# A two-layer decoder step: GpSimd's splits in pieces of 128 columns, the sample's SSD step in full tiles, no GpSimd work around the second norm

## The chip, the cores and the metric

The kernel runs on one core of one Trainium2 chip. The metric is the device time of one execution in microseconds (us). A core has engines that run their own instruction streams and wait for each other on semaphores: TensorE (PE in the profile; PEld is its loading of weights), VectorE (DVE), ScalarE (ACT), GpSimd (POOL) and SyncE (SP), whose queue issues almost all of the DMA transfers here.

## The reference

One inference step of a decoder of two layers, for a prompt of 1024 tokens and 8 sample sequences of one token each, whose 8192 past tokens lie in a paged cache. Cut to what matters:

```
def trunk_layer(x, c, ...):
    shift1, scale1, gate1, shift2, scale2, gate2 = split(silu(c) @ w_ada + b_ada)
    h = rmsnorm(x, g_norm1) * (1 + scale1) + shift1
    z, xbc, dt_raw, cq, ckv, kpe, u = split(h @ w_in)
    ssd_out, hT, conv_new = ssd_mixer(z, xbc, dt_raw, conv_buf, h0, ...)   # 6 heads x 64, state 128, 2 groups
    mla_out = rmsnorm(attend(q, lat, kpe_r), g_mla_out)                     # latent attention, 6 heads
    pool_out, pool_new = pool_mixer(u, pool_buf, ...)
    x = x + gate1 * (concat(ssd_out, mla_out, pool_out) @ w_out)
    h2 = rmsnorm(x, g_norm2) * (1 + scale2) + shift2
    x = x + gate2 * ((silu(h2 @ w_gate) * (h2 @ w_up)) @ w_down)            # 1024 -> 2816 -> 1024
    return x, lat, kpe_r, hT, conv_new, pool_new
```

For a sample sequence the SSD step is one token long: the new state is exp(dt A) h0 + B (dt x), the output is C times the new state, plus D x. All arithmetic is float32.

## The kernel before

Activations lie transposed, features on the 128 partitions and the 1032 tokens (1024 of the prompt, then the 8 of the sample) in columns. A float32 product is made of three matmuls: each operand is cut into a high part that ScalarE rounds (line 88) and the rest, which VectorE or GpSimd makes by a subtraction (line 89, or 1141 for the cached pages); `gemm` and `mm3` then sum high x high, low x high and high x low (lines 133 to 135). So each weight tile and each activation tile that TensorE uses costs one ScalarE copy and one subtraction, and the constants at the end of the file say which subtractions GpSimd makes.

Each layer has these stages, with the times of layer 0 in the profiled execution: the first norm and the input projection (0 to 270 us); a weave (270 to 990) of generators that take turns: `sample` (the attention of the eight sample sequences over their pages, split by `smp_split` in tiles of 4 x 128 columns), and beside it one after another `ssd_prompt`, `ssd_sample`, `ssd_finish` and `mla_prompt`, and blocks of the adaLN product; the output projection and the second norm (990 to about 1200); the up passes of the FFN with a seven-product scheme (to 1600); the down passes (to 1845). Layer 1 repeats this.

`ssd_sample` takes the eight sequences in four steps (two groups g, two halves q of four sequences). A step scales the old state by a decay (line 668, on GpSimd), adds the outer product of B and dt x (line 665, operands of 8 rows), and `product` multiplies the new state with one column of C for each sequence (lines 637 to 641, one column streamed).

`out_proj` goes over the two halves g of the tokens, and in each over eight tiles m of the output features: it loads the weight tile i + 2 and splits tile i + 1 ahead (`out_load`, `out_conv`; OPV lists the tiles that VectorE splits, GpSimd the others), multiplies, adds the gated result to x (line 1411), squares it and sums the squares (line 1423, GpSimd where m is even). `norm_half` makes the second norm of half g: `fresh` multiplies four of the tiles by the reciprocal root (line 1457) and applies scale and shift column block by column block (line 1462 on VectorE for the blocks in XFV, line 1465 on ScalarE for the others); `cut` splits them into X for the FFN (on GpSimd for the blocks in XPL); sums and differences of blocks follow (line 1481). It runs for half 0 while `out_proj` works on half 1. `up_first` loads the first up and gate weights and prepares WAH = 3 of their operands; `up_conv` prepares one (sums of blocks at line 1538, on GpSimd for those in WPS in the first four passes and in WPT later; then a split, on GpSimd for those in WPF and WPL). The first four passes take one half of the tokens each, the later ones both.

Tiles come from two pools: `C` gives one of NA = 24 slots of 128 x 1032, `B` one of 20. A tile that finds no free slot waits until an older one is released. The Tile framework schedules each engine's instructions; the order follows the order of issue in the text with priorities, so the engines' order can change with the change.

Of the kernel before, what the change touches and what calls it, by code (L numbers as in the profile page):

```python
# [17 lines left out]
TP = 1024  # L18
NB = 8
# [29 lines left out]
class Net:  # L49
# [36 lines left out]
    def split(self, x, h, l, eng=None):  # L86
        nc = self.nc
        nc.scalar.copy(h, x)  # L88
        (eng or nc.gpsimd).tensor_tensor(out=l, in0=x, in1=h.bitcast(F32), op=ALU.subtract)  # L89
# [345 lines left out]
    def softplus(self, l):  # L435
# [43 lines left out]
        ea = self.ea = self.S([6, NB], "ea", bufs=1)  # L479
        nc.scalar.activation(out=ea, in_=p[0:6, 128 - NB:128], func=AF.Exp)  # L480
# [5 lines left out]
    def ssd_prompt(self, l):  # L486
# [9 lines left out]
        def decays(c):  # L496
# [10 lines left out]
            for g in range(2):  # L507
# [14 lines left out]
                if c:  # L522
                    nc.scalar.activation(out=E[:, 384 * g:384 * g + 384], in_=df[:, 0:384], func=AF.Exp)
                    (nc.gpsimd if g in PE6 else nc.vector).tensor_tensor(
                        out=e6[:, 3 * g:3 * g + 3, :], in0=e6[:, 3 * g:3 * g + 3, :],
                        in1=Cf[g][:, s].unsqueeze(1).to_broadcast([128, 3, 128]), op=ALU.mult)
# [10 lines left out]
        for c in range(8):  # L537
# [9 lines left out]
            for g in range(2):  # L547
                (nc.gpsimd if g in PM6 else nc.vector).tensor_tensor(
                    out=m6[:, 3 * g:3 * g + 3, :], in0=m6[:, 3 * g:3 * g + 3, :],
                    in1=gm[:, g, :].unsqueeze(1).to_broadcast([128, 3, 128]), op=ALU.mult)  # L550
# [44 lines left out]
    def ssd_sample(self, l):  # L595
# [7 lines left out]
        for h in range(6):  # L603
            nc.tensor.matmul(p[:, NB * h:NB * h + NB], self.K(K_ID + h, 1, r1=6).to_broadcast([6, 128]), ea,
                             start=True, stop=True)
        px = self.Gp()
        for i in range(3):
            for e in range(2):
                nc.tensor.matmul(px[64 * e:64 * e + 64, NB * i:NB * i + NB],
                                 self.K(K_ID + 64 + 2 * i + e, 1, 64, 70).to_broadcast([6, 64]), acr[64:70, TP:],  # L610
                                 start=True, stop=True)
        eb = self.S([128, 6, NB], "eb", bufs=1)
        nc.vector.tensor_copy(eb, p[:, 0:48].rearrange("p (h b) -> p h b", h=6))
        xd = self.S([128, 3, NB], "xd", bufs=1)
        for i in range(3):
            nc.vector.tensor_tensor(out=xd[:, i, :], in0=x[i][:, TP:], in1=px[:, NB * i:NB * i + NB],
                                    op=ALU.mult)
        yield 3
        p = self.Gp()
        for i in range(3):  # L620
            nc.tensor.transpose(p[0:NB, 128 * i:128 * i + 128], xd[:, i, :], self.K(K_ID, 128))
        xn = self.C(name="xnb")[0:NB, 0:384]
        nc.vector.tensor_copy(xn, p[0:NB, 0:384])
        p = self.Gp()
        for g in range(2):
            nc.tensor.transpose(p[0:NB, 128 * g:128 * g + 128], Bf[g][:, TP:], self.K(K_ID, 128))
        bn = self.C(name="bnb")[0:NB, 0:256]
        nc.vector.tensor_copy(bn, p[0:NB, 0:256])
        yield 3
        ysb = self.S([128, 24], "ysb", bufs=1)  # L630
        def product(g, q, h1):
            yp = self.Gp()
            for b in range(4):
                o = 192 * b
                cc = Cf[g][:, TP + 4 * q + b:TP + 4 * q + b + 1]
                if g == 0:
                    nc.tensor.matmul(yp[:, b:b + 1], h1[:, o:o + 128], cc, start=True, stop=True)
                    nc.tensor.matmul(yp[0:64, 4 + b:5 + b], h1[:, o + 128:o + 192], cc, start=True, stop=True)
                else:
                    nc.tensor.matmul(yp[64:128, b:b + 1], h1[:, o:o + 64], cc, start=True, stop=True)  # L640
                    nc.tensor.matmul(yp[:, 4 + b:5 + b], h1[:, o + 64:o + 192], cc, start=True, stop=True)
            for j, r, a in (((0, slice(0, 128), 0), (1, slice(0, 64), 4)) if g == 0 else
                            ((1, slice(64, 128), 0), (2, slice(0, 128), 4))):
                nc.vector.tensor_copy(ysb[r, 8 * j + 4 * q:8 * j + 4 * q + 4], yp[r, a:a + 4])

        pend = None
        def state(i):
# [5 lines left out]
        for g in range(2):  # L653
            for q in range(2):

                rhs, h1 = self.C(name="hr"), self.C(name="h1")
                if g + q < 2:
                    state(2 * g + q + 1)
                nc.vector.tensor_tensor(
                    out=rhs[0:NB, 0:768].rearrange("p (b e) -> p b e", b=4),  # L660
                    in0=xn[:, 192 * g:192 * g + 192].unsqueeze(1).to_broadcast([NB, 4, 192]),
                    in1=self.K(K_ID + 4 * q, 4, r1=NB).unsqueeze(2).to_broadcast([NB, 4, 192]), op=ALU.mult)
                d = [self.Gp() for _ in range(2)]
                for a in range(2):
                    nc.tensor.matmul(d[a][:, 0:384], bn[:, 128 * g:128 * g + 128], rhs[0:NB, 384 * a:384 * a + 384],
# [18 lines left out]
        yield  # L684
        for j in range(3):
            nc.vector.scalar_tensor_tensor(out=self.y[j][:, TP:], in0=x[j][:, TP:], scalar=self.V(l, V_DSK + j),
                                           in1=ysb[:, 8 * j:8 * j + 8], op0=ALU.mult, op1=ALU.add)
# [443 lines left out]
    def smp_split(self, page):  # L1131
# [9 lines left out]
        nc.gpsimd.tensor_tensor(out=ll, in0=v, in1=lh.bitcast(F32), op=ALU.subtract)  # L1141
# [229 lines left out]
    def out_proj(self, l, mod, xsrc, side):  # L1371
# [6 lines left out]
        for i, (g, m) in enumerate(todo):  # L1378
# [7 lines left out]
            if g:  # L1386
                for _ in range(SDO):
                    next(side[0], None)
            if i == 1:
# [32 lines left out]
            else:  # L1422
                (nc.vector if m % 2 else nc.gpsimd).tensor_tensor(out=sqs[z], in0=sqs[z], in1=sq, op=ALU.add)
# [136 lines left out]
    def up_first(self, l):  # L1560
# [5 lines left out]
        for j in range(WAH):  # L1566
            self.up_conv(l, j)

    def ffn(self, l, X, mod, side, sink):
# [10 lines left out]
        done = WAH + WA0  # L1580
        for j in range(7 * len(self.passes)):
            while done <= j + WAH:
# [428 lines left out]
```

## Time and profile before

| | |
|---|---|
| time, median of 3 runs | 3662.61 us (3662.19 to 3663.1) |
| the profiled execution's own time | 3663.35 us |
| its span in the profile | 3661.6 us |
| busy: TensorE, VectorE, ScalarE, GpSimd | 3436.4, 2358.1, 1732.6, 1546.8 us |
| mean granted clock of TensorE | 0.962 |
| GpSimd instructions | 1173 |

The profile is of one execution, and its span leaves 1.75 us of that execution's time outside. Busy times count each engine alone; the engines work side by side. The clock is that of TensorE as a share of 2.4 GHz, of which 0.5 is the lower of its two levels.

### The profile page before, as it was taken

Reading aid. Unit: us, or ns where it says so; the run is one execution under the profiler, and the core shown is the slowest. Engines: PE = TensorE matmul, PEld = TensorE weight load, DVE = VectorE, ACT = ScalarE, POOL = GpSimd, SP = SyncE. Lnnn points to the kernel's source line nnn. Section 1 sums busy time; section 2 is a strip of 40 time slices with the busy share of each in tenths; the row PEclk is TensorE's granted clock in tenths of the full one; section 3 lists DMA queues with packets and bytes.
Section 4 is the critical chain, followed back from the end, with each engine's and each line's share of the span. In section 5 each row is a group of like instructions: output and inputs, shape, how many; then the busy total and the mean of one; then the engine's idle time right before and its main releaser. Section 6 shows DMA issues by size and latency. Waiting matters only on the chain. (4 is left out here: it accounts for less than half of the span.)

```text
span 3661.6 us, 66619 instructions
## 1 busy us (share of the span) xinstructions
PE 3436.4 (94%) x23740; PEld 3091.1 (84%) x23740; DVE 2358.1 (64%) x4308; ACT 1732.6 (47%) x4455; POOL 1546.8 (42%) x1173
## 2 busy tenths in 40 slices
PE   8988989899997999999999899998998979999999
PEld 6977767677787999999999776677777979999999
DVE  4568686778878555542345687777877685555433
ACT  4227466777844333331132365777776443333220
POOL 2225444444244655543222254445453455555431
PEclk9999799999998999999999998999999989999999
DMA  5234555544442222142222255554443522222432
GB/s 199 47 83 146 167 180 174 157 139 117 142 143 86 86 80 86 72 173 89 81 77 61 81 168 174 176 149 112 125 126 109 159 79 82 77 81 81 170 97 70
DMA packets 255322, 430.10 MB, mean 117 GB/s; under 512 B 38736, under 2 KB 180944, under 8 KB 254992
## 3 DMA queue, kind: packets, MB, share of 16 engines
q1 hardware_dynamic: 246800, 409.04, 35.2%
q0 software_dynamic: 8192, 16.79, 1.8%
q8 instruction: 190, 3.11, 0.4%
q14 instruction: 140, 1.15, 0.1%
HBM read 372.84 MB, written 52.87 MB: 116 GB/s over the span
## 5 line engine op out<-in xcount | busy, mean ns | idle before, releaser
L1158 ACT ACTIVATE sqk<-psd 128x384 f32<-128x384 f32 x1024 | 497.6, 503 | 234.2 <-PE psd L135 184.5
L1141 POOL TENSOR_TENSOR lt<-pg,lt 128x512 fp32r<-128x512 f32 x256 | 311.3, 1224 | 544.1 <-ACT lt L1140 426.5
L1305 DVE TENSOR_REDUCE ss<-sqk 128x12 f32<-128x768 f32 x448 | 421.3, 943 | 127.0 <-ACT sqk L1158 125.7
L133 PE MATMUL psd<-mv,lt 128*128 128x390 f32 x1024 | 439.8, 429 | 7.0 <-ACT scr L1159 6.9
L134 PE MATMUL psd<-X,wp 128*128 128x258 f32 x1408 | 400.9, 285 | 3.2 <-DVE wp L89 3.2
L133 PE MATMUL psd<-X,wp 128*128 128x258 f32 x1408 | 401.2, 285 | 0.0
L135 PE MATMUL psd<-X,wp 128*128 128x258 f32 x1408 | 400.8, 285 | 0.0
L134 PE MATMUL psd<-mv,lt 128*128 128x390 f32 x1024 | 369.6, 361 | 5.9 <-POOL lt L1141 5.9
L135 PE MATMUL psd<-mv,lt 128*128 128x390 f32 x1024 | 367.8, 359 | 0.0
L134 PE MATMUL psg<-X,wp 128*128 128x258 f32 x1056 | 302.9, 287 | 35.4 <-DVE wp L89 35.4
L135 PE MATMUL psg<-X,wp 128*128 128x258 f32 x1056 | 302.2, 286 | 0.0
L133 PE MATMUL psg<-X,wp 128*128 128x258 f32 x1056 | 301.8, 286 | 0.0
L1093 POOL DMA_INDIRECT kp<-kpeT,kidx x256 | 249.1, 973 | 124.2 <-issue 91.6
L133 PEld LDWEIGHTS psd<-mv,lt 128*128 128x128 f32 x1024 | 204.4, 200 | 105.4 <-issue 46.4
L89 POOL TENSOR_TENSOR wl<-wr,wh 128x1024 fp32r<-128x1024 f32 x47 | 125.7, 2679 | 374.5 <-ACT wh L88 288.3
L134 PEld LDWEIGHTS psd<-X,wp 128*128 128x128 f32 x1408 | 269.5, 191 | 3.5 <-DVE wp L89 3.5
L133 PEld LDWEIGHTS psd<-X,wp 128*128 128x128 f32 x1408 | 269.9, 192 | 0.0
L133 PE MATMUL psd<-op,wh 128*128 128x348 f32 (+1 forms) x792 | 252.6, 319 | 18.1 <-DVE pb L419 9.5
L135 PEld LDWEIGHTS psd<-X,wp 128*128 128x128 f32 x1408 | 269.6, 191 | 0.0
L134 PE MATMUL psd<-op,wl 128*128 128x348 f32 (+1 forms) x792 | 251.0, 317 | 10.5 <-DVE wl L89 5.7
L135 PE MATMUL psd<-op,wh 128*128 128x348 f32 (+1 forms) x792 | 249.8, 317 | 1.8 <-POOL op L89 1.4
L89 POOL TENSOR_TENSOR wp<-wr,wp 128x512 fp32r<-128x512 f32 x128 | 167.1, 1306 | 198.5 <-ACT wp L88 194.0
(466 smaller groups left out, 9898.6 us busy)
## 6 DMA issues: line engine op xcount, KB each, us to landing
pg<-pages SPq DMA_DIRECT2D x1024, 129.0 KB
wa<-wada SPq DMA_DIRECT2D x96, 512.0 KB
wr<-wff SPq DMA_DIRECT2D x96, 512.0 KB
ar<-actd SPq DMA_DIRECT2D x44, 516.0 KB
actd<-G SPq DMA_DIRECT2D x40, 516.0 KB
wd<-wdn SPq DMA_DIRECT2D x48, 384.0 KB
wr<-win SPq DMA_DIRECT2D x32, 512.0 KB
wr<-wout SPq DMA_DIRECT2D x32, 512.0 KB
```

The source lines that it names most:

```text
L89: (eng or nc.gpsimd).tensor_tensor(out=l, in0=x, in1=h.bitcast(F32), op=ALU.subtract)
L133: nc.tensor.matmul(ps, wh, xh, start=start, stop=False)
L134: nc.tensor.matmul(ps, wl, xh, start=False, stop=False)
L135: nc.tensor.matmul(ps, wh, xl, start=False, stop=stop)
L1093: self.nc.gpsimd.indirect_dma_start(out=kts[-1][:, 128 * g:128 * g + 128], out_offset=None, in_=self.A["kpeT"], in_offset=bass.IndirectOff ...
L1141: nc.gpsimd.tensor_tensor(out=ll, in0=v, in1=lh.bitcast(F32), op=ALU.subtract)
L1158: nc.scalar.activation(out=sq, in_=d[:, kc], func=AF.Square)
L1305: nc.vector.tensor_reduce(out=o, in_=x, axis=AX.X, op=ALU.add)
```

## The change

Three edits are made together. (1) Every subtraction that GpSimd makes in `split` and in `smp_split`, and its products of 3 x 128 columns in `ssd_prompt` (lines 524 and 548), become several instructions of 128 or 129 columns (PCE = 129): four for 512 or 516 columns, six for 768, eight for 1024 or 1032. The sums at lines 1538 and 1423, the state's scaling at 668 and all VectorE work stay whole. (2) `ssd_sample` works with 128 rows: decays, dt x, B and C are taken with the last 128 tokens or with zeros around the eight sequences, `product` streams 192 columns of the state against a 128 x 128 tile that is zero but for one column of C and sums four of them in PSUM, and three transposes bring the result back. (3) Around the second norm GpSimd loses the splits of X, of the up weights in the first four passes and of the output projection's weights for half 1, and the sums of squares of half 1; scale and shift go to ScalarE whole. `up_first` moves into tile m = 3 of half 0 of `out_proj`, and tiles 4 to 7 prepare two up weights each, so that eight are ready where three were.

```diff
     def split(self, x, h, l, eng=None):
         nc.scalar.copy(h, x)
-        (eng or nc.gpsimd).tensor_tensor(out=l, in0=x, in1=h.bitcast(F32), op=ALU.subtract)
+        if eng is None or eng is nc.gpsimd:
+            n = x.shape[-1]
+            for a in range(0, n, PCE):
+                c = slice(a, min(n, a + PCE))
+                nc.gpsimd.tensor_tensor(out=l[:, c], in0=x[:, c], in1=h[:, c].bitcast(F32), op=ALU.subtract)
+        else:
+            eng.tensor_tensor(out=l, in0=x, in1=h.bitcast(F32), op=ALU.subtract)
...
-        ea = self.ea = self.S([6, NB], "ea", bufs=1)
-        nc.scalar.activation(out=ea, in_=p[0:6, 128 - NB:128], func=AF.Exp)
+        ea = self.ea = self.S([128, NB], "ea", bufs=1)
+        nc.gpsimd.memset(ea, 0.0)
+        nc.scalar.activation(out=ea[0:6], in_=p[0:6, 128 - NB:128], func=AF.Exp)
...
+                    if g in PE6:
+                        for h in range(3 * g, 3 * g + 3):
+                            nc.gpsimd.tensor_tensor(out=e6[:, h, :], in0=e6[:, h, :], in1=Cf[g][:, s], op=ALU.mult)
...
+        t = self.C(name="xnb")
+        xn, bn, xd = t[:, 0:384], t[:, 384:640], t[:, 640:1024].rearrange("p (i x) -> p i x", i=3)
+        nc.gpsimd.memset(xd, 0.0)
+        for h in range(6):
+            r = slice(64 * (h % 2), 64 * (h % 2) + 64)
+            nc.vector.tensor_tensor(out=xd[r, h // 2, 128 - NB:], in0=x[h // 2][r, TP:],
+                                    in1=px[r, NB * h:NB * h + NB], op=ALU.mult)
+        zs = [self.C(name="zc") for _ in range(2)]
+        for z, cf in zip(zs, Cf):
+            nc.gpsimd.memset(z, 0.0)
+            nc.vector.tensor_copy(z[:, 0:129 * NB].rearrange("p (b x) -> p b x", x=129)[:, :, 0], cf[:, TP:])
...
-            for b in range(4):
-                o = 192 * b
-                cc = Cf[g][:, TP + 4 * q + b:TP + 4 * q + b + 1]
-                if g == 0:
-                    nc.tensor.matmul(yp[:, b:b + 1], h1[:, o:o + 128], cc, start=True, stop=True)
-                    nc.tensor.matmul(yp[0:64, 4 + b:5 + b], h1[:, o + 128:o + 192], cc, start=True, stop=True)
...
+            for b in range(4 * q, 4 * q + 4):
+                o = 192 * (b - 4 * q)
+                nc.tensor.matmul(yp[:, 0:192], zs[g][:, 128 * b:128 * b + 128], h1[:, o:o + 192], start=b == 4 * q,
+                                 stop=b == 4 * q + 3)
...
-                nc.tensor.matmul(d[a][:, 0:384], bn[:, 128 * g:128 * g + 128], rhs[0:NB, 384 * a:384 * a + 384],
+                nc.tensor.matmul(d[a][:, 0:384], bn[:, 128 * g:128 * g + 128], rhs[:, 384 * a:384 * a + 384],
...
+        p = self.Gp()
+        for j in range(3):
+            nc.tensor.transpose(p[:, 128 * j:128 * j + 128], yb[:, 128 * j:128 * j + 128], self.K(K_ID, 128))
...
-        nc.gpsimd.tensor_tensor(out=ll, in0=v, in1=lh.bitcast(F32), op=ALU.subtract)
+        for a in range(4):
+            nc.gpsimd.tensor_tensor(out=ll[:, a], in0=v[:, a], in1=lh[:, a].bitcast(F32), op=ALU.subtract)
...
+            elif m == UF0:
+                self.up_first(l)
+            elif m > UF0:
+                for _ in range(UFN):
+                    self.up_ahead(l)
...
-                (nc.vector if m % 2 else nc.gpsimd).tensor_tensor(out=sqs[z], in0=sqs[z], in1=sq, op=ALU.add)
+                (nc.vector if g or m % 2 else nc.gpsimd).tensor_tensor(out=sqs[z], in0=sqs[z], in1=sq, op=ALU.add)
...
-        for j in range(WAH):
-            self.up_conv(l, j)
+        self.done = 0
+
+    def up_ahead(self, l):
+        self.up_conv(l, self.done)
+        self.done += 1
...
-WPT, WPL, XPT, XPL, GUP = (0, 1, 2, 3), (0, 2, 4, 6), (), (1, 5, 7), 0
+WPT, WPL, XPT, XPL, GUP = (0, 1, 2, 3), (0, 2, 4, 6), (), (), 0
+UF0, UFN = 3, 2
-XFV, WPF, WPS, OPV = (1, 3), (2,), (0, 1), (0, 2, 4, 6, 8, 10, 12, 14)
+XFV, WPF, WPS, OPV = (), (), (), (0, 2, 4, 6, 8, 9, 10, 11, 12, 13, 14, 15)
-PGR, PH = 0, 1
+PGR, PH, PCE = 0, 1, 129
```

## Rows read from the trace of the kernel before

**Rows 1.** The page, part 1: busy us (share of the span), instructions.
```profile
PE 3436.4 (94%) x23740; PEld 3091.1 (84%) x23740; DVE 2358.1 (64%) x4308; ACT 1732.6 (47%) x4455; POOL 1546.8 (42%) x1173
```

**Rows 2.** Windows by stage: length, busy us (instructions) by engine, clock, DMA, GB/s.
```profile
270.00:990.00 720.00, 668.78 (x4333) 522.12 (x4333) 550.31 (x1059) 504.08 (x1594) 322.00 (x303) 0.95 0.50 150
990.00:1200.00 210.00, 176.60 (x1330) 170.83 (x1330) 175.93 (x265) 100.73 (x203) 89.92 (x48) 0.89 0.38 127
1200.00:1600.00 400.00, 398.51 (x3320) 397.94 (x3318) 227.26 (x356) 138.45 (x275) 220.45 (x156) 1.00 0.22 79
```

**Rows 3.** Waits of PE, whole run: line, releaser: us, times, longest.
```profile
PE psg L134 <- DVE wp L89: 35.4, 7, 8.6
PE psg L853 <- DVE rx L839: 12.2, 4, 3.2
...
PE psd L133 <- DVE pb L419: 9.5, 2, 5.7
...
PE psd L134 <- POOL lt L1141: 5.9, 4, 2.2
```

**Rows 4.** Timelines of POOL and DVE near 1079 us: start, length, operation.
```profile
1079.36 2.37 POOL L89 TENSOR_TENSOR X<-xb,X 128x1032 fp32r<-128x1032 f32 x1 [5.59 <-ACT X L88]
...
1079.46 2.42 DVE L1462 TENSOR_SCALAR xb<-xb,gs,mod 128x258 f32<-128x258 f32 x1
...
1081.88 0.41 DVE L1462 TENSOR_SCALAR xb<-xb,gs,mod 128x258 f32<-128x258 f32 x1
```

**Rows 5.** Timelines of POOL and DVE at 388 and at 874 us.
```profile
387.57 1.95 POOL L668 TENSOR_TENSOR h<-h,eb 128x192 f32<-128x192 f32 x4 [1.07 <-DMA h<-sssm]
...
388.28 0.39 DVE L1179 TENSOR_TENSOR scr<-scr,kr 128x96 f32<-128x96 f32 x1
...
874.62 4.60 POOL L1141 TENSOR_TENSOR lt<-pg,lt 128x512 fp32r<-128x512 f32 x4
...
874.25 5.01 DVE L1222 TENSOR_SCALAR wd<-kt,cw 6x6 f32<-6x6 f32 x1
```

**Rows 6.** Windows over ssd_sample, in both layers.
```profile
393.00:410.00 17.00, 17.00 (x57) 14.59 (x58) 6.51 (x15) 4.13 (x14) 5.04 (x9) 0.50 0.37 119
413.00:432.00 19.00, 17.43 (x90) 14.36 (x91) 11.64 (x28) 7.53 (x19) 8.77 (x9) 0.64 0.90 281
2208.00:2240.00 32.00, 32.00 (x142) 26.70 (x141) 15.00 (x38) 8.93 (x32) 13.32 (x16) 0.57 0.58 180
```

**Rows 7.** Timeline of PE in ssd_sample.
```profile
390.38 1.55 PE L665 MATMUL psg<-hr,bnb 8*128 8x384 f32 x4 [0.33 <-DVE hr L659]
391.86 0.38 PE L637 MATMUL psg<-cv,h 128*128 128x1 f32 x2
...
394.08 0.37 PE L638 MATMUL psg<-cv,h 128*64 128x1 f32 x2
```

**Rows 8.** Groups of POOL's instructions by shape, whole run.
```profile
L1141 POOL TENSOR_TENSOR lt<-pg,lt 128x512 fp32r<-128x512 f32 x256 | 311.3, 1224 | 544.1 <-ACT lt L1140 426.5 <-DMA pg<-pages 66.7 <-PE psm L1111 16.5
...
L89 POOL TENSOR_TENSOR wl<-wd,wh 128x768 fp32r<-128x768 f32 x48 | 90.4, 1887 | 174.7 <-ACT wh L88 102.9 <-PE psg L134 28.9 <-DVE ac L89 15.3
```

**Rows 9.** Waits of POOL, 270 to 990 us.
```profile
POOL lt L1141 <- ACT lt L1140: 211.5, 58, 13.4
```

**Rows 10.** Windows around the second norm, layer 0.
```profile
1123.00:1195.00 72.00, 52.65 (x361) 51.52 (x360) 67.32 (x95) 35.29 (x64) 32.06 (x17) 0.81 0.26 87
...
1030.00:1077.00 47.00, 46.92 (x381) 46.38 (x382) 28.84 (x42) 17.17 (x34) 18.97 (x11) 1.00 0.53 175
```

**Rows 11.** Groups of DVE's instructions by shape, 1123 to 1195 us.
```profile
L89 DVE TENSOR_TENSOR wp<-wr,wp 128x512 fp32r<-128x512 f32 x15 | 12.4, 848 | 0.1
...
L89 DVE TENSOR_TENSOR X<-xb,X 128x1032 fp32r<-128x1032 f32 x4 | 7.0, 1754 | 0.0
L1624 DVE TENSOR_TENSOR G<-G,U 128x516 f32<-128x516 f32 x3 | 5.9, 1980 | 0.1
...
L1462 DVE TENSOR_SCALAR xb<-xb,gs,mod 128x258 f32<-128x258 f32 x4 | 4.6, 1158 | 0.0
```

More of the change, by code (lines that the diff above doesn't have):

```diff
@@ L547, in ssd_prompt @@
             for g in range(2):
-                (nc.gpsimd if g in PM6 else nc.vector).tensor_tensor(
-                    out=m6[:, 3 * g:3 * g + 3, :], in0=m6[:, 3 * g:3 * g + 3, :],
-                    in1=gm[:, g, :].unsqueeze(1).to_broadcast([128, 3, 128]), op=ALU.mult)
+                if g in PM6:
+                    for h in range(3 * g, 3 * g + 3):
+                        nc.gpsimd.tensor_tensor(out=m6[:, h, :], in0=m6[:, h, :], in1=gm[:, g, :], op=ALU.mult)
+                else:
+                    nc.vector.tensor_tensor(
+                        out=m6[:, 3 * g:3 * g + 3, :], in0=m6[:, 3 * g:3 * g + 3, :],
+                        in1=gm[:, g, :].unsqueeze(1).to_broadcast([128, 3, 128]), op=ALU.mult)
             yield
@@ L603, in ssd_sample @@
         for h in range(6):
-            nc.tensor.matmul(p[:, NB * h:NB * h + NB], self.K(K_ID + h, 1, r1=6).to_broadcast([6, 128]), ea,
+            nc.tensor.matmul(p[:, NB * h:NB * h + NB], self.K(K_ID + h, 1).to_broadcast([128, 128]), ea,
                              start=True, stop=True)
         px = self.Gp()
[L607 to L611, printed above, removed]
+        for h in range(6):
+            nc.tensor.matmul(px[:, NB * h:NB * h + NB], self.K(K_ID + 64 + h, 1).to_broadcast([128, 128]), acr[:, TP:],
+                             start=True, stop=True)
         eb = self.S([128, 6, NB], "eb", bufs=1)
         nc.vector.tensor_copy(eb, p[:, 0:48].rearrange("p (h b) -> p h b", h=6))
[L614 to L617, printed above, removed]
+        t = self.C(name="xnb")
+        xn, bn, xd = t[:, 0:384], t[:, 384:640], t[:, 640:1024].rearrange("p (i x) -> p i x", i=3)
+        nc.gpsimd.memset(xd, 0.0)
+        for h in range(6):
+            r = slice(64 * (h % 2), 64 * (h % 2) + 64)
[5 more added lines that the diff above has]
+            nc.vector.tensor_copy(z[:, 0:129 * NB].rearrange("p (b x) -> p b x", x=129)[:, :, 0], cf[:, TP:])
         yield 3
@@ L620, in ssd_sample @@
         for i in range(3):
[L621 to L623 removed]
+            nc.tensor.transpose(p[:, 128 * i:128 * i + 128], xd[:, i, :], self.K(K_ID, 128))
+        nc.vector.tensor_copy(xn, p[:, 0:384])
         p = self.Gp()
         for g in range(2):
[L626 to L628 removed]
+            nc.tensor.transpose(p[:, 128 * g:128 * g + 128], Bf[g][:, T - 128:], self.K(K_ID, 128))
+        nc.vector.tensor_copy(bn, p[:, 0:256])
         yield 3
[L630 removed]
+        yb = xd.rearrange("p i x -> p (i x)")
         def product(g, q, h1):
             yp = self.Gp()
[L633 to L644 removed]
+            for b in range(4 * q, 4 * q + 4):
+                o = 192 * (b - 4 * q)
+                nc.tensor.matmul(yp[:, 0:192], zs[g][:, 128 * b:128 * b + 128], h1[:, o:o + 192], start=b == 4 * q,
+                                 stop=b == 4 * q + 3)
+            o = yb[:, 192 * g:192 * g + 192]
+            if q:
+                nc.vector.tensor_tensor(out=o, in0=o, in1=yp[:, 0:192], op=ALU.add)
+                zs[g] = None
+            else:
+                nc.vector.tensor_copy(o, yp[:, 0:192])
         pend = None
@@ L1579, in ffn @@
         last = self.passes[-1][0]
-        done = WAH + WA0
         for j in range(7 * len(self.passes)):
-            while done <= j + WAH:
-                self.up_conv(l, done)
-                done += 1
+            while self.done <= j + WAH:
+                self.up_ahead(l)
             n, i = divmod(j, 7)
@@ L1804, in build @@
             gs = n.norm_gain(l, mod, 4, V_GN2)
-            n.up_first(l)
             side[0] = n.norm_half(0, mod, gs, 3, X)
@@ L1809, in build @@
                 pass
-            for j in range(WA0):
-                n.up_conv(l, WAH + j)
+            for _ in range(WA0):
+                n.up_ahead(l)
             side = n.norm_half(1, mod, gs, 3, X)
```

15 lines of the change are left out of this document (8 added, 7 removed).

## The prediction

> **What bounds the kernel now.** I read the page first: busy shares of the engines [rows 1]. The reader is to see TensorE (PE) at 94% of the span, so about 225 us of the 3661.6 are idle, and everything this change can win lies there or in matmuls that run at less than full clock. Then I cut the span into its stages [rows 2]: the weave of the sample's attention with the SSD work (270 to 990 us, and again in layer 1) leaves PE 51 us idle at clock 0.95, the stretch of output projection and second norm (990 to 1200) leaves 33 us idle at clock 0.89, and in the FFN's up passes PE is busy 398.5 of 400 us at clock 1.00. So the FFN stages can gain nothing, and only two kinds of stretch per layer are open. Third, the waits of PE over the whole run [rows 3]: the largest is for a VectorE (DVE) part of an up weight, 35.4 us in 7 waits; those for rx, the largest among several small DVE results of the prompt's attention and the sample's, come to 12.2, those for pb in the input projection to 9.5, and waits for GpSimd's (POOL) page split lt only to 5.9. DVE is late, POOL nearly never.
>
> Why DVE is late, the timelines show. A 128x258 DVE operation that takes 0.41 us elsewhere took 2.42 while POOL ran a 2.37 us subtraction beside it, and it ended when that one ended [rows 4]. So a DVE operation of this kind is held for the rest of a POOL operation. The question for the pieces is whether it comes in at the end of one POOL instruction or only when POOL's queue runs dry, and the rows say both [rows 5]: under four back-to-back 192-column POOL products a DVE operation took 0.39 us, so it got in; under four back-to-back 512-column subtractions a tiny one (6x6) was held 5.01 us, through all four.
>
> **The clock in ssd_sample.** The stage runs at clock 0.95 as a whole; in 393 to 410 it is 0.50 with PE busy all 17 us, in 413 to 432 it is 0.64, in layer 1's 2208 to 2240 it is 0.57 [rows 6]. 0.50 is the lower of the two levels, 1.2 GHz. What PE did before the fall: matmuls of 8 rows, then eight one-column products (each two records in the trace), from 391.86 to 394.4, 2.5 us [rows 7]. The change turns both into full tiles: 128 rows instead of 8, four matmuls of 192 columns instead of eight of one. Lost at the lower clock: 17 x 0.5 = 8.5, 17.43 x 0.36 = 6.3, 32 x 0.43 = 13.8, together 28.6 us. Some of it is not lost to the clock alone (the stage has other waits, PE 93% busy there), so I take 22, with bounds 0 and 30. The product itself: eight products in 2.5 us become four matmuls of half the columns of L665's, of which two (four records) take 1.55 us; so about 1.6 instead of 2.5, some 1 us each, eight in all, mostly inside the same stretches; it pays for what is added: three more transposes, three more DVE products, the zero fills on POOL (two of 1032 columns and one of 384 a layer, each no longer than a subtraction of as many, 2.37 us [rows 4]; POOL waits for ScalarE (ACT) 211.5 us in the stage [rows 9], which hides them; without that cover up to 5.6 us a layer). I set the added work at 2 us beyond this, between 0 and 6.
>
> **The second norm.** In the 72 us from 1123 to 1195 PE is busy 52.65 us at clock 0.81, so at full clock its work is about 43 us; DVE is busy 67.3 of the 72, POOL 32.1 [rows 10]. That is a DVE-bound stretch, and its operations are longer than alone [rows 11]: X splits 1754 ns for 1.23, wp 848 for 0.68, the 258-column scalings 1158 for 0.41, G x U 1980 for about 0.67. Over their counts that is 2.1 + 2.5 + 3.0 + 3.9 us; with some 6.5 for the rest (scalings of 250 columns, other weight parts, the products and differences of 1032 columns) 18 us of holds. The change takes POOL away here. What DVE gets in its place: three X splits (1.15 us each, a little less than their length, since DVE operations overlap at the ends) and, by the constants of the code, one split and two sums in each of the four first passes at 0.6 us: 3.5 + 7. What it loses: eight scalings go to ACT (2.6 us) and the preparation of five more weights moves ahead into the first half of the output projection (about 4.8), where DVE is busy only 28.8 of 47 us [rows 10]. Net +3 of work for 18 of holds: 15 us off 72. ACT now makes the four scalings one after another (about 0.6 us each), which delays each new X by a microsecond or two; so 12 a layer, 24 in all. Bounds: nothing, and all that PE's 43 us leave, 29 a layer.
>
> **The pieces elsewhere.** A DVE operation now waits at best for a 128-column piece, about a quarter of a 1.2 us page split [rows 8], where it waited for a 1.2 to 2.4 us instruction. But POOL's work is the same in sum, so the holds become shorter and more frequent: this takes away the long waits, not the lock. Of PE's waits for small DVE results, of which rx with 12.2 us is the largest [rows 3], I credit 8 us for both layers (bounds 0 and 20). In the input projection (the pb wait) and in the early output projection the same mechanism gives 4 and 2, together 6 (bounds 0 and 12).
> What the pieces cost POOL: four 192-column products take 1.95 us back to back [rows 5], one 768-column subtraction 1.89 [rows 8]. So an instruction more costs about 0.02 us; for some 2300 more pieces 46 us on an engine that is busy 42%. On the path nothing; PE's waits for lt are 5.9 us in the whole run [rows 3].
> The Trainium skill (GPSIMD Engine Reference, section 3.1) speaks against pieces: it gives each GpSimd instruction two software dispatch hops where DVE's one costs about 156 ns. By that 2300 pieces would cost POOL some 360 us, an estimate from that page. The rows of four against one contradict it for instructions that are queued back to back.
>
> **Slots.** From the code: the general pool has 24 slots of a 128x1032 tile, and in the second half of the output projection I count 23 of them taken before the change (eight xb, weights, sums, loads). Five more up weights are then held there. The loads move too: up_first puts two of 512 KB on SP's queue at the fourth tile of the first half, the fourth weight's preparation two more, all ahead of the out-projection's own loads of the later tiles; a load that waits for a slot holds those behind it, an out-projection weight and the residual input xt among them. Then these come later, and PE may wait at some tiles. What one tile pays without look-ahead is a DVE subtraction of 1024 columns, 1.2 us as the X splits alone [rows 11], behind an ACT copy of the same columns, for which I take 1.0, no load counted: 2.2. I put in 8 us, between 0 and all 32 tiles at 2.2, 70.
>
> **Sum.** 22 + 24 + 8 + 6 - 2 - 8 = 50 us against this execution's own 3663.35 (span 3661.6 and 1.75 around it): 3613.35. The median of the runs, 3662.61, lies 0.74 below it: 3613 rounded.
>
> **The rivals.**
> 1. The lock does not pass between queued pieces: POOL's pieces of one split are issued with nothing between them, as the four 512-column subtractions that held a 6x6 operation for 5.01 us [rows 5]. For it: that row; against: the 0.39 us one. Then the 14 us of the pieces' terms go but for a microsecond or two: 3626.
> 2. The clock falls all the same: PE was busy in these stretches, and if the fall comes not from these thin operands but from the other small matmuls of the weave around them, full tiles do not hold it. Then the 22 go: 3635. The Trainium skill (TensorE: Matmul & The Clock Gate, "What's actually happening") says that the gate follows how busy PE has been. By that alone a new form that keeps PE as busy as the old one changes nothing here, which would be the same 3635; the rows, with the clock at 0.50 while PE was busy all 17 us, do not bear it out in this simple form.
> 3. Slower: the slots. The five weights held early push the out-projection's weights out of look-ahead, and PE stalls at each of its 16 tiles a layer. At 2.2 us a tile that is 70 us instead of my 8: 3675. It decides from about 1.8 us a tile: 32 x 1.8 = 58, the 50 of gain and the 8 already in. For it: 23 of 24 slots; against: that DVE is free there and loads wait on slots only as early as they are asked for.
> 4. POOL late: its page splits take longer in pieces and PE waits for lt. If one in ten of its 256 splits is late by half a microsecond, that is 13 us: 3626. Against: POOL waits 211.5 us for ACT in one such stage [rows 9]. The dispatch price of the page above speaks for it.
> 5. Gains lie beside other waits, as the stage waits for ACT next: within a few us of before, 3659.
>
> **How the numbers follow.** Likeliest case 0.46, lock not passed 0.18, clock unchanged 0.14, slots 0.11, POOL late 0.05, no gain 0.06. What a measurement tells from no change is 0.2%, 7 us: below 3655 is faster, above 3670 slower. The first three and POOL late make 0.83; a little of these falls to no change: faster 0.81, same 0.08, slower 0.11. The range goes at the low end to the upper bounds of two terms together (30 for the clock instead of 22, 40 for the second norm instead of 24, and 10 more of the pieces: 34 us, 3579), at the high end past the clock rival with the lock rival in it (3648): 3578 to 3654. The slots and the gainless case, 0.17, stay out above.
>
> **What the profile after would show.** Right: clock 1.00 where ssd_sample's products run, no stretch of 17 us at 0.50; no POOL instruction over about 0.7 us but the unpieced ones; no DVE scalings (L1462) left in the second norm; from the end of the output projection to the end of the fourth pass about 60 us instead of 72; PE's wait for wp from 35 us to under 15. Wrong: DVE operations of 96 columns that still last 1 to 4 us under a row of pieces; clock 0.50 after full-tile products; PE waiting in the output projection for wl or wh at tile after tile, with SP waiting for tiles of the pool.

## The result and the profile after

The changed kernel takes 3614.85 us (median of 4 runs, 3612.53 to 3619.1), the kernel before 3662.4 in the same comparison: ratio 0.9871, 95% interval 0.9854 to 0.9888, so some 47 us faster. 3613 was predicted. The span of its profile is 3613.6 us, 48.0 less than before.

The page's busy times, to be read beside [rows 1]: POOL is not less but more busy, by 313 us, although it lost work; DVE has 84 us less.

```profile
PE 3403.6 (94%) x23682; PEld 3057.7 (85%) x23682; DVE 2273.8 (63%) x4328; ACT 1741.4 (48%) x4487; POOL 1859.9 (51%) x3346
```

The windows by stage, then the 72 us from the end of the second norm's sums and the last 31 us of the output projection before it:

```profile
270.00:990.00 720.00, 661.19 (x4345) 515.31 (x4345) 556.93 (x1083) 509.81 (x1624) 405.60 (x790) 0.97 0.51 155
990.00:1200.00 210.00, 185.00 (x1453) 178.72 (x1454) 154.29 (x269) 105.60 (x203) 69.81 (x108) 0.93 0.36 117
...
1116.00:1188.00 72.00, 63.27 (x481) 60.79 (x480) 61.31 (x105) 41.72 (x80) 20.88 (x27) 0.95 0.26 90
1085.00:1116.00 31.00, 26.40 (x193) 25.99 (x194) 15.45 (x27) 8.36 (x14) 0.00 (x0) 0.89 0.40 121
```

Beside [rows 2] the sample's stage has clock 0.97 for 0.95 and PE does no more work in its 720 us; the stretch from 990, where the work is now some 10 us further on, has 185 us of PE work for 176.6. In the 72 us DVE is busy 61.3 us where it was 67.3 [rows 10], and PE 63.3 for 52.7. Its splits of X take 1233 ns each where [rows 11] has 1754:

```profile
L95 DVE TENSOR_TENSOR X<-xb,X 128x1032 fp32r<-128x1032 f32 x7 | 8.4, 1233 | 0.0
```

But in the 31 us before, with POOL at rest and DVE busy only half the time, PE stands 4.6 us idle at clock 0.89: something there is not DVE.

Waits of PE over the whole run:

```profile
PE psg L912 <- DVE m L906: 16.2, 5, 5.3
...
PE psd L139 <- DVE pj L291: 10.3, 2, 5.2
...
PE psg L140 <- DVE wp L95: 7.1, 7, 2.1
PE psg L876 <- DVE rx L862: 6.4, 4, 1.9
...
PE psd L140 <- POOL lt L1165: 5.0, 4, 2.3
...
PE psg L140 <- POOL wl L93: 2.0, 2, 1.0
...
PE psd L140 <- POOL wl L93: 0.3, 1, 0.3
```

and four rows of the same view of the kernel before, which [rows 3] leaves out:

```profile
PE psd L134 <- POOL wl L89: 7.7, 5, 2.0
PE psg L134 <- POOL wl L89: 5.6, 2, 2.8
PE psg L889 <- DVE m L883: 4.1, 5, 0.9
PE psd L133 <- DVE pj L285: 1.2, 2, 0.6
```

Beside [rows 3] the wait for wp fell from 35.4 to 7.1 (from 3.2 to 4.2 in the psd group), that for rx from 12.2 to 6.4; lt, 5.9 before, is 5.0. The wait for pb is gone, but pj, one step on in the same stage, holds PE for 10.3 where pb and pj made 10.7 together; m, in the prompt's attention, holds it for 16.2 where it was 4.1. And a wait that nobody had looked at is nearly gone: PE waited 13.3 us for GpSimd's own low part of a weight (wl, 7.7 and 5.6), and now waits 2.3.

Where the 48 us went is read off the starts of PE's operations, stage by stage (first and last page product, first outer product of the states, last matmul of ssd_finish, first and last up product):

| stretch, us | before, layers 0 and 1 | after | sum of changes |
|---|---|---|---|
| to the first page product (layer 1: from the last up product) | 269.0, 489.3 | 267.5, 481.9 | -8.9 |
| to the first outer product | 117.8, 115.8 | 119.6, 121.3 | +7.3 |
| to the end of ssd_finish | 62.8, 61.6 | 51.8, 51.8 | -20.8 |
| to the last page product | 549.7, 536.7 | 549.9, 531.1 | -5.4 |
| to the first up product | 125.2, 127.6 | 129.5, 132.2 | +8.9 |
| to the last up product | 471.1, 471.1 | 456.9, 456.8 | -28.5 |
| to the end | 263.9 | 263.2 | -0.7 |

In ssd_sample the clock, in the 40 us from the first outer product of each layer, in the kernel before and in the changed one:

```profile
387.00:427.00 40.00, 39.67 (x175) 32.48 (x174) 19.42 (x47) 11.44 (x41) 18.09 (x24) 0.62 0.61 183
...
2201.00:2241.00 40.00, 38.62 (x175) 31.23 (x174) 20.79 (x48) 11.81 (x42) 18.08 (x24) 0.66 0.65 203
```

```profile
387.00:427.00 40.00, 33.38 (x173) 25.78 (x173) 33.21 (x64) 16.41 (x50) 29.38 (x51) 0.91 0.65 205
...
2178.00:2218.00 40.00, 32.92 (x181) 25.17 (x181) 33.52 (x64) 17.32 (x54) 30.62 (x52) 0.96 0.65 210
```

and the product itself, eight records where there were sixteen, 1.51 us for the 2.5 of [rows 7]:

```profile
387.06 1.56 PE L685 MATMUL psg<-hr,xnb 128*128 128x384 f32 x4 [0.81 <-DVE hr L679]
...
390.86 1.51 PE L656 MATMUL psg<-h,zc 128*128 128x192 f32 x8
```

The reader is to see the DVE column (the third pair) too: 33 of 40 us, where it was 19 to 21. PE stands idle 6.6 us in layer 0 where it stood idle 0.3: the clock no longer sets the pace there, other engines do, DVE the busiest of them. One fall to 0.50 is left inside the first window, of 6.8 us from 416.0. PE has just stood still for 4.2 us there, and this is what it waited for (POOL and DVE by their timelines, then the wait over the whole run):

```profile
410.17 5.72 POOL L1165 TENSOR_TENSOR lt<-pg,lt 128x128 fp32r<-128x128 f32 x12
...
410.34 5.24 DVE L717 TENSOR_TENSOR cv<-cv,pj 128x1032 f32<-128x1032 f32 x1
...
PE psg L731 <- ACT ysq L719: 8.0, 2, 4.2
```

A DVE product of 1032 columns, 1.22 us long when nothing holds it, took 5.24 beside twelve pieces of page splits, and 4.80 in layer 1; ACT's square and PE's sum wait behind it, 8.0 us for both layers, where the same wait was 3.3 us before. In the second profile of the changed kernel the product meets no such row and the wait is 0.5 us.

What a piece costs: the page splits by their line, before and after, with minimum, median and maximum in ns.

```profile
L1141 POOL TENSOR_TENSOR lt<-pg,lt x256: 1172/1193/2232, 265.1 to 2779.9; 128x512 fp32r<-128x512 f32 x128
...
L1165 POOL TENSOR_TENSOR lt<-pg,lt x1024: 399/448/1447, 263.9 to 2743.4; 128x128 fp32r<-128x128 f32 x171
```

Four make 1.79 us where one whole split took 1.19: 0.60 us for three more instructions, 0.20 each, not 0.02. And does the lock pass between queued pieces? First POOL and DVE near 1594 us, then near 1032 us:

```profile
1594.51 3.45 POOL L93 TENSOR_TENSOR ac<-ar,ac 128x129 fp32r<-128x129 f32 x8
1597.93 5.12 POOL L93 TENSOR_TENSOR wl<-wd,wh 128x129 fp32r<-128x129 f32 x12
1603.02 3.44 POOL L93 TENSOR_TENSOR ac<-ar,ac 128x129 fp32r<-128x129 f32 x8
1606.43 2.56 POOL L93 TENSOR_TENSOR wl<-wd,wh 128x129 fp32r<-128x129 f32 x6
...
1594.14 14.48 DVE L1360 TENSOR_TENSOR x<-x,rs 128x8 f32<-128x8 f32 x1
```

```profile
1031.62 4.80 POOL L93 TENSOR_TENSOR wl<-wr,wh 128x129 fp32r<-128x129 f32 x7 [5.35 <-ACT wh L88]
...
1033.40 0.95 DVE L95 TENSOR_TENSOR wp<-wr,wp 128x512 fp32r<-128x512 f32 x1
```

At 1594 a DVE operation of 8 columns is held 14.48 us, through 33 pieces that follow each other without a gap. At 1033 a 512-column subtraction under seven pieces takes 0.95 us, 0.27 more than alone: it waited for one piece at most. The second is the usual case. Take the DVE operations that start while a POOL operation on tiles runs (reductions and operations with a PSUM source left out), and take off the time of each the undisturbed time of its line and shape (the one that a tenth of them stay under). The median of what is left fell from 0.74 to 0.12 us at up to 16 columns, from 0.60 to 0.12 at 17 to 129, from 0.68 to 0.21 at 259 to 516, and from 1.00 to 0.14 above; at 130 to 258, most of them in the up passes beside the 512-column sums of line 1538 that stay whole, it did not fall (0.48, 0.64). The nine longest holds left, from 4.3 us to the 14.3 here, hit operations of at most 96 columns; the two after them are the 1032-column products above, 4.0 and 3.6 us.

### The profile page after: what moved, and what is told of

It reads as the page before. It is cut to its first block, busy times and chain, and to the rows that moved or that the text cites. A ratio compares the mean times of both kernels' runs of the same rounds, so it can differ in the third digit from the quotient of the medians.

```text
span 3613.6 us, 68353 instructions
## 1 busy us (share of the span) xinstructions
PE 3403.6 (94%) x23682; PEld 3057.7 (85%) x23682; DVE 2273.8 (63%) x4328; ACT 1741.4 (48%) x4487; POOL 1859.9 (51%) x3346
## 5 line engine op out<-in xcount | busy, mean ns | idle before, releaser
L1165 POOL TENSOR_TENSOR lt<-pg,lt 128x128 fp32r<-128x128 f32 x1024 | 441.1, 464 | 421.4 <-ACT lt L1163 371.7
L139 PE MATMUL psd<-mv,lt 128*128 128x390 f32 x1024 | 431.5, 421 | 4.6 <-ACT scr L1183 4.5
L140 PE MATMUL psd<-mv,lt 128*128 128x390 f32 x1024 | 359.1, 351 | 5.0 <-POOL lt L1165 5.0
L141 PE MATMUL psd<-mv,lt 128*128 128x390 f32 x1024 | 358.0, 350 | 0.0
L93 POOL TENSOR_TENSOR wl<-wr,wh 128x129 fp32r<-128x129 f32 (+1 forms) x312 | 170.6, 583 | 304.3 <-ACT wh L88 232.5
L93 POOL TENSOR_TENSOR wp<-wr,wp 128x129 fp32r<-128x129 f32 x480 | 263.7, 580 | 103.7 <-ACT wp L88 99.8
L139 PE MATMUL psd<-op,wh 128*128 128x348 f32 (+1 forms) x792 | 251.4, 319 | 24.0 <-DVE pj L291 10.3
```

Source lines behind the costliest of these rows:

```text
L93: nc.gpsimd.tensor_tensor(out=l[:, c], in0=x[:, c], in1=h[:, c].bitcast(F32), op=ALU.subtract)
L139: nc.tensor.matmul(ps, wh, xh, start=start, stop=False)
L140: nc.tensor.matmul(ps, wl, xh, start=False, stop=False)
L141: nc.tensor.matmul(ps, wh, xl, start=False, stop=stop)
L1165: nc.gpsimd.tensor_tensor(out=ll[:, a], in0=v[:, a], in1=lh[:, a].bitcast(F32), op=ALU.subtract)
```

## The experiments

They ran on other chips than the first result, on which the kernel before takes 3743 to 3756 us, nearly all of the difference in the stage of the sample's attention; so each kernel is given by its ratio to the kernel before on its own chip, and by stretches outside that stage, which differ little between chips. From the last page product to the first up product, and from there to the last, the changed kernel again takes 129.5 and 456.9 us in layer 0, as in its first profile, and 128.7 and 457.7 in layer 1, for 132.2 and 456.8. Six profiles with the same code in the output projection lie between 127.7 and 132.2, so 3 us in one layer of one profile mean little.

**One part alone, or all but the pieces.** Each part of the diff on the kernel before; and the changed kernel with whole POOL instructions.

```diff
# changed, no pieces (in words):
-PGR, PH, PCE = 0, 1, 129
+whole subtractions in split and smp_split, whole products at lines 524 and 548
```

> Only the pieces, all else as before. Theory of the prediction: they shorten DVE's holds in the sample's stage and the projections, 14 us less, 3648. Reading of the trace after: the stages outside ssd_sample and the second norm lose only about 8 us (input projections) and the sample's stage nothing, 3654. Rival, the pieces' own cost on POOL (448 ns a piece, 1.8 us for four where one took 1.2) makes it late: 3662 or more.

> Only ssd_sample in full tiles, all else as before. Theory: the clock holds at 1.00 through the products and the stage from the first state to the end of ssd_finish becomes 10 to 11 us shorter a layer, so 20 to 22 in all, 3641. Rival: the clock holds only because DVE and POOL are also faster there; then the gain is under 10, over 3652.

> Only the second norm's part (no GpSimd work there and eight up weights prepared ahead). Theory: 14 us less a layer from the end of the second norm's sums to the last up pass, 4 to 5 more in the output projection, so 19 to 20 less in all, 3643. Rival: the gain needs the pieces also, since POOL still works at the edges; then under 10 less, over 3652.

> The changed kernel with whole GpSimd instructions. If the pieces are worth 8 us (input projections) it runs in 3622; if they are worth the 14 of the prediction, 3629; if their cost on POOL eats their gain, 3614 or less.

| kernel | ratio to before | interval | last page to last up product, layers 0 and 1 |
|---|---|---|---|
| pieces alone | 0.9927 | 0.9911 to 0.9943 | 589.2, 593.5 |
| full tiles alone | 0.9982 | 0.9969 to 0.9995 | 595.2, 599.0 |
| second norm's part alone | 0.9956 | 0.9941 to 0.9971 | 591.6, 587.2 |
| changed, no pieces | 0.9950 | 0.9934 to 0.9966 | 591.7, 589.1 |

On that chip's 3752.66 us the parts are worth 27, 7 and 17 us, 51 in sum; with intervals of 5 to 6 us each they add up. The pieces give more than either theory said, and the last row says the same: without them the changed kernel gains 19 us in place of some 45, so all three sums of its expectation were too early. The full tiles give a third of what was expected, so in time their rival came true, but not by its reason: with all else as before the clock over the 40 us is 0.95 and 0.98, and the stretch to the end of ssd_finish is 6 to 9 us a layer shorter than in the two kernels of this chip that keep both thin forms. The norm's part gives nearly what was expected, though not where: the up passes are 14 us a layer shorter, the output projection 10 and 2 us longer.

```profile
394.00:434.00 40.00, 32.65 (x173) 25.31 (x171) 33.17 (x62) 16.35 (x50) 24.94 (x30) 0.95 0.64 199
...
2245.00:2285.00 40.00, 31.77 (x177) 24.46 (x181) 32.47 (x64) 16.49 (x52) 26.65 (x31) 0.98 0.64 206
```

Of the 27 us of the pieces, 21 lie outside the sample's stage: 12 from the last page product to the last up product (596.3 and 598.7 before), 9 in the input projections and down passes. In these 9 the wait that went is PE's for GpSimd's wl: 10.7 us there in the kernel before, 2.2 with the pieces alone, while the waits for pb and pj together stayed near 10. In the kernels with whole instructions (second norm's part alone; changed, no pieces) the wl waits of the whole run are 11.7 and 10.6 us. One such place in the input projection of layer 0, before and in the changed kernel:

```profile
227.37 4.48 POOL L89 TENSOR_TENSOR wl<-wr,wh 128x1024 fp32r<-128x1024 f32 x1 [26.77 <-DVE pb L403]
...
231.90 0.43 PE L134 MATMUL psg<-op,wl 128*128 128x348 f32 x1 [2.78 <-POOL wl L89]
```

```profile
227.67 5.56 POOL L93 TENSOR_TENSOR wl<-wr,wh 128x129 fp32r<-128x129 f32 x8 [23.31 <-DVE pb L409]
...
230.32 0.43 PE L140 MATMUL psg<-op,wl 128*128 128x348 f32 x1 [0.98 <-POOL wl L93]
```

Before, PE's first product with this wl starts when the whole subtraction has ended; with pieces it starts 2.9 us before the last piece ends, since each product reads 128 columns of wl. So the pieces shorten the projections mostly by letting PE start on a part of the tile, and not by DVE's holds.

**The page splits whole.** The four-line loop over `ll[:, a]` is one subtraction again, all other pieces stay; and the changed kernel itself beside it.

> The changed kernel once more, as the measure for the other kernels of this chip: 1.3% under the kernel before. From the end of the sample's pages to the first up product some 130 us, the up passes 457, as in its first profile.

> The changed kernel with the page splits of the sample's attention whole again, all other pieces kept. By the prediction these pieces are worth 8 us in the sample's stage: 8 us longer. By the stages of the two profiles they are worth nothing there: within 4 us of the changed kernel, or a little shorter, since POOL does 311 us in place of 441.

The changed kernel again: 0.9882 (0.9859 to 0.9905). With whole page splits: 0.9871 (0.9852 to 0.9890). So the kernel with whole page splits is some 6 us shorter, within the noise of both; 8 us longer, as by the prediction, lies just outside it. The pieces of the page splits, 768 of the 2300 or so, give nothing that shows.

**What makes the clock fall.** The changed kernel with one of the two thin forms back, then with both.

```diff
 # e5: the one-column product
-                nc.tensor.matmul(yp[:, 0:192], zs[g][:, 128 * b:128 * b + 128], h1[:, o:o + 192], ...)
+                nc.tensor.matmul(yp[:, b:b + 1], h1[:, o:o + 128], cc, start=True, stop=True)
 # e6: the outer product with 8 rows
-                nc.tensor.matmul(d[a][:, 0:384], bn[:, ...], rhs[:, 384 * a:384 * a + 384], ...)
+                nc.tensor.matmul(d[a][:, 0:384], bn[0:NB, ...], rhs[0:NB, 384 * a:384 * a + 384], ...)
 # e10: ssd_sample as before, both
```

> The changed kernel with the one-column products back, its outer product still with 128 rows. If the one-column products make the clock fall: 0.50 stretches after them, and 8 to 10 us a layer longer from the first state to the end of ssd_finish, 16 to 20 in all. Rival, the 8-row operands make it fall: clock 1.00 there, and only some 2 us a layer for the products' own length.

> The changed kernel with the 8-row outer product back (and the 6-row broadcasts), its product in full tiles. If the one-column products alone make the clock fall: clock 1.00 and the time of the changed kernel within 3 us. Rival, the 8-row operands do: 0.50 stretches, 16 to 20 us longer.

> The changed kernel with ssd_sample as before, 8-row operands and one-column products. If the clock falls only where both are thin, the 0.50 stretches of some 17 and 14 us come back and the stretch from the first state to the end of ssd_finish is 63 us a layer, with 7 to 14 us in all lost against the changed kernel. Rival, the pieces or the second norm alone hold the clock: no such stretches, no loss.

The same 40 us from the first outer product, both layers of each: thin product only, thin rows only, both.

```profile
391.00:431.00 40.00, 35.28 (x193) 28.43 (x192) 27.20 (x57) 15.94 (x50) 24.50 (x44) 0.83 0.69 217
...
2220.00:2260.00 40.00, 34.03 (x192) 27.58 (x191) 26.96 (x57) 16.02 (x50) 25.49 (x45) 0.87 0.67 217
```

```profile
387.00:427.00 40.00, 34.33 (x173) 26.66 (x171) 28.79 (x62) 15.90 (x50) 28.77 (x50) 0.91 0.68 213
...
2210.00:2250.00 40.00, 35.12 (x171) 27.60 (x171) 28.49 (x60) 15.84 (x50) 27.11 (x50) 0.87 0.68 213
```

```profile
388.00:428.00 40.00, 39.68 (x175) 32.31 (x174) 18.99 (x46) 11.86 (x43) 20.63 (x38) 0.62 0.59 178
...
2228.00:2268.00 40.00, 39.74 (x175) 32.53 (x175) 19.13 (x47) 11.50 (x42) 20.29 (x37) 0.62 0.58 182
```

With both the clock is 0.62 in both layers, as before the change; the two kernels above that keep both (pieces alone, second norm's part alone) have 0.62 to 0.74. With either one alone it is 0.83 to 0.91, with both filled 0.91 to 0.98 in all runs. Ratios: 0.9870 (0.9848 to 0.9891), 0.9876 (0.9854 to 0.9898), and 0.9888 (0.9861 to 0.9914) with both. So in time e5 came out nearer its rival and e6 as its first theory, which contradict each other if one form alone makes the clock fall: the fall of 14 to 17 us over the products comes where 8-row matmuls and one-column products stand in turn, and filling either takes it away. Filling one does not take all: e5 still has 13.7 us at 0.50 in layer 0, from 25 us after its first outer product, with PE busy 82% of it; why is open.

And the whole edit, judged by e10, is worth less here than can be measured: the falls of 17 and 14 us came back, the 7 to 14 us in all did not show, and an effect of some 10 us would be hidden by the intervals. The stretch from the first outer product to the end of ssd_finish is 62.9 and 63.6 us with both thin forms and 59.7 and 56.6 in the second profile of the changed kernel; of those 10 us the stretch before gives 5 back (121.2 and 120.6 against 123.3 and 123.5, most likely for the zero fills and wider copies).

**The early up weights, and who works at the second norm.** In e8 `up_first` and its three weights stand where they stood before; e11 gives half of the scalings back to DVE; e12 on top of that gives POOL the odd output-projection splits of half 1 in pieces.

```diff
 # e8
-            elif m == UF0:
-                self.up_first(l)
-            elif m > UF0: (two up_ahead)
+            n.up_first(l)     # after half 0, three weights
 # e11
-XFV, WPF, WPS, OPV = (), (), (), (0, 2, 4, 6, 8, 9, 10, 11, 12, 13, 14, 15)
+XFV, WPF, WPS, OPV = (1, 3), (), (), (0, 2, 4, 6, 8, 9, 10, 11, 12, 13, 14, 15)
 # e12
+XFV, WPF, WPS, OPV = (1, 3), (), (), (0, 2, 4, 6, 8, 10, 12, 14)
```

> The changed kernel with the loads and the preparation of the up weights in their old place: three weights before half 1 instead of eight in half 0. If the early weights (slots, SP's queue) are what makes the output projection 4.5 us a layer longer, that stretch falls from 129 us to 125 and the up passes grow by more: 457 to over 462, in sum 2 to 10 us longer than the changed kernel. Rival, they are worth nothing: both stretches as in the changed kernel.

> The changed kernel with half of the second norm's scalings on VectorE again. In the changed kernel PE waits in the output projection for ACT's high part of a weight (wh), 6.3 us in four waits. If ACT's four scalings in a row make that, these waits fall under 2 us and the output projection by 3 to 5 us a layer, 6 to 10 us shorter in all. Rival, DVE needs the room: up passes longer by as much.

> As the one before, and GpSimd makes every second output-projection split of half 1 again, in pieces. With the pieces only, the output projection took 121 us; if POOL in pieces disturbs DVE little, the stretch falls by another 2 to 4 us a layer. Rival, POOL beside DVE costs in the second norm what it saves: no shorter than with half of the scalings alone.

| kernel | ratio to before | interval | last page to first up | first up to last up |
|---|---|---|---|---|
| without early weights (e8) | 0.9824 | 0.9805 to 0.9842 | 117.7, 117.5 | 459.5, 460.1 |
| half of the scalings on DVE (e11) | 0.9852 | 0.9830 to 0.9874 | 129.9, 129.9 | 457.8, 458.4 |
| and POOL in half 1 (e12) | 0.9909 | 0.9892 to 0.9925 | 134.1, 132.9 | 459.6, 458.7 |

e8 beats both kernels: 0.9824 means 66 us off the kernel before, with an interval below that of the changed kernel. Its first theory, 2 to 10 us longer, and its rival, no change, are both wrong. Against the second profile of the changed kernel the output projection is 12 and 11 us shorter and the up passes 3 and 2 longer, so the early weights cost 9 us a layer; against e10, on the same chip and with the same code there, 7. The waits show part of how. First PE's waits for ACT's high part of an output-projection weight, in the changed kernel and in e8 (windows around the projection):

```profile
PE psd L139 <- ACT wh L88: 4.0, 2, 3.0
PE psg L139 <- ACT wh L88: 2.3, 2, 1.4
```

```profile
PE psg L139 <- ACT wh L88: 1.1, 1, 1.1
```

Then ACT in the changed kernel, and SP's waits in half 1 there and in e8 (whose line 1423 is line 1428 of the changed kernel):

```profile
1077.24 1.05 ACT L88 CAST X<-xb 128x1032 fp32r<-128x1032 f32 x1
1082.12 1.06 ACT L88 CAST X<-xb 128x1032 fp32r<-128x1032 f32 x1 [3.83 <-DVE xb L1510]
...
1084.66 1.03 ACT L88 CAST wh<-wr 128x1024 fp32r<-128x1024 f32 x1
...
1088.11 1.04 ACT L88 CAST wh<-wr 128x1024 fp32r<-128x1024 f32 x1 [0.82 <-DMA wr<-wout]
```

```profile
SPq L1428 <- DVE wl L95: 5.1, 1, 5.1
SPq L1428 <- DVE xb L1445: 4.8, 1, 4.8
SPq L1428 <- DVE rv L100: 2.4, 1, 2.4
SPq L129 <- DVE wp L95: 2.1, 1, 2.1
```

```profile
SPq L1423 <- PE psg L141: 1.5, 1, 1.5
SPq L1423 <- DVE wl L95: 0.7, 1, 0.7
```

ACT stood 3.83 us for a norm difference of DVE (xb, line 1510) with the copy of the next output-projection weight behind it in its queue, and the copy after that waited for the weight's load. SP's load of xt, line 1428, and of weights, line 129, waited for releases by DVE, 14.4 us in these four rows; in e8 two such waits are left, 2.2 us. Read so, those are loads held for a slot. A rival stands: the early preparation is itself 7 us more of DVE work in the projection of layer 0 (busy 88.5 us, in e8 81.2), and no run keeps that work there without the loads. e11 took half of the scalings from ACT: PE's waits for wh in the projection fell from 6.3 us to 3.9, not under 2, and the stretch stayed at 129.9, so neither its theory nor its rival came true (the up passes are 1 us longer), and ACT's row of scalings alone does not explain the cost. In e12 its rival held: with POOL back at work in half 1 the stretch is 4 and 3 us longer than in e11, above all six profiles named before, and the kernel 19 us.

## Why the prediction came out right

The whole came out within 2 us, and that closeness is luck: the mechanisms of the clock and of the second norm were right, those of the pieces only in part, several terms were mis-sized, and they cancelled.

- **The clock** (22 us, less 2 for the added work). The long fall went, as forecast, and with full tiles alone too (e2), so the second rival fell. The stretch lost 20.8 us in the first profile. The mis-sized term is the added work, set at 2: the stretch before grew by 7.3, which leaves 13.5, and PE at full clock stands idle 6.6 of 40 us. By e2 the edit is worth 7 us on another chip, by e10 nothing that shows. The sum took 22 of the 28.6 us at the lower clock as gain, and did not ask what comes next there: DVE, busy 33 of 40 us. That DVE sets the pace is read from its busy time and from the held product, and no run tests it. The cause "thin operands" was too broad: the long fall over the products needs both forms together, shown by e5, e6 and e10. The Trainium skill's rule that I had weighed (TensorE: Matmul & The Clock Gate, "What's actually happening": the gate follows how busy PE has been) does not hold here in the plain form: in e10 PE was busy 39.7 of 40 us at 0.62.
- **The second norm** (24) and **the slots** (-8). The mechanism held: DVE is faster where POOL does not work beside it (an X split 1.23 us for 1.75), and from the first up product to the end of the fourth pass layer 0 takes 54.2 us where it took 68.9, 14.7 less for the 12 forecast. Net 16 was said; 19.6 is measured from the last page product to the last up product, of which the pieces alone make 7 and 5 in the two layers (e1). In the first profile both terms look right one by one, 28.5 less in the up passes and 8.9 more before them; that is luck again. The early weights cost 18 us for both layers (15 against e10), not 8, and without them the whole stretch gains 40, pieces included. The rival of the slots was real in kind, a quarter of the 70 us it was given, and it did not decide. That SP's waits for slots are the cause was argued from the waits; a larger pool was not tried, so the shares of ACT's order and of the moved DVE work in it stay open.
- **The pieces** (8 in the sample's stage, 6 in the projections). The sizes look right in the first profile, 5.4 less in the sample's stage after ssd_finish and 9.6 in the projections with the down passes, but the reason given holds only for a part. In the sample's stage the wait for rx fell by 6 us, with the pieces alone too (6.4, against 12.2 with whole instructions), but the wait for m grew by 12, and e9 shows nothing for the page splits' own pieces. In the projections the pb wait, which the term was taken from, only changed its name to pj; what went is PE's wait for GpSimd's wl. The prediction had read "POOL nearly never" from the wait for lt alone and passed over 13.3 us of wl. Alone the pieces are worth 27 us, more than 14, 12 of it in the stretch around the second norm where the sum had the norm's edit take all.
- **The first rival**, that the lock does not pass, was true of a few operations (14.48 us) and false of most, by the medians above. Twice in the first profile it cost PE time, the 8.0 us behind the held products of ssd_finish.
- **POOL's cost**: 0.02 us for an instruction more was wrong, 0.20 us is measured. The pieces alone make POOL 470 us busier with 2379 instructions more (e1), where 46 was said; in the changed kernel it is 313, because POOL also lost work. The step that failed set four 192-column products against one 768-column subtraction, another kind of operation: the products take some 0.5 us each, hardly more than a 128-column piece. The Trainium skill (GPSIMD Engine Reference, section 3.1), which I set against the rows, gives some 156 ns for a dispatch on DVE and more hops on GpSimd, and the estimate from it, 360 us, was the nearer. The rows decided wrongly; it cost PE no time at the page splits, where its waits for lt stayed at 5.0.

## What to carry to other kernels

Short GpSimd instructions cost 0.20 us for each one more, and can give two things: VectorE is held for less time in the median, and TensorE can start on the first columns of a tile before the last are done. Look in the waits for either one before cutting: pieces of weights paid here, pieces of page splits, for which TensorE hardly waits, did not. Work moved ahead holds slots and stands in the queues of VectorE, ScalarE and SP: measure the stretch that it moves into, not only the one it leaves. When edits are bundled, run each alone and take each out: here a part of one edit took back 18 us that nobody saw in a faster total.

## What was not expected of the hardware

A VectorE operation of 8 columns waited 14.48 us while 33 GpSimd pieces ran one after another, others of 6 to 96 columns 4.3 to 6 us, and two of 1032 columns some 4 us, while the operations of 512 columns near 1033 us came in after one piece. The Trainium skill (SBUF — State Buffer, "Who interferes with whom") says that a VectorE instruction with two SBUF inputs contends with a GpSimd instruction that reads SBUF, and that issue order, not the operation's shape, decides who blocks. That fits the four longest holds and those of 1032 columns, which all have two such inputs (a cast of 6 columns, held 4.6 us, has one); but no row tells why a waiting operation loses 33 times in a row, and no run here settled it. And the clock of TensorE was 0.62 over 40 us with PE busy 39.7 of them where 8-row matmuls and one-column products alternate, and 0.83 or more where one of the two was filled.
